# A fourth buffer for gathered rows during the gate-table stage, in the place of two extra raw buffers of U

## The chip, the cores and the metric

The kernel runs on one core of a Trainium2 chip. The metric is device time in microseconds (us). TensorE multiplies matrices (it takes its work from one sequencer, weight loads and matmuls in a row), VectorE and ScalarE work element by element, GpSimd here starts gathers, and SyncE's queue (SP) starts plain loads. Each engine works off its instructions in order.

## The reference, cut to what matters

One decoder layer on 528 tokens: a mixer (attention and mLSTM) and then a PEER layer, in which each token picks 128 of 16384 experts and uses a row of U and a row of V (2048 numbers each) of each expert:

```python
    idx = jnp.take_along_axis(cand_i, best_pos, axis=-1).reshape(T, PEER_HEADS * PEER_TOPK)
    gate = jax.nn.softmax(best_s, axis=-1).reshape(T, PEER_HEADS * PEER_TOPK).astype(h.dtype)
    ...
        ub = jnp.take(u, ib, axis=0)
        act = jax.nn.gelu(jnp.einsum('td,tkd->tk', hb, ub), approximate=False)
        return jnp.einsum('tk,tkd->td', gb * act, jnp.take(v, ib, axis=0))
```

## The kernel before

The PEER layer is done in two ways at once. For 352 tokens (ND) all 16384 experts are computed densely on TensorE: U is read in 128 chunks of 1 MB and multiplied, and a table of gates (zero but for the 128 picked experts) then weighs the result before it is multiplied with V. For the last 160 tokens the picked rows are gathered instead: GpSimd starts an indirect DMA that fetches one row per partition (128 rows of 8 KB, 1 MB), and VectorE multiplies it with the token's vector (rows of U) or adds it to a sum (rows of V). These are the 320 jobs of the list `jobs`, in the order d (128), D (32), A (32), a (128).

A chunk of U comes in two halves of 512 KB. `split_half` (L76 to L82) takes each apart for exact products: the load `raw` on SP's queue (L73), a cast `hi` on ScalarE (L80), and the subtraction `lo = raw - hi` on VectorE (L81), which is the last reader of `raw`. A chunk has 16 k-steps of three matmuls (L90 to L92: hi, lo, hi); the first half serves steps 0 to 7, the second 8 to 15. `step` (L888) first calls `uload` for the chunk after, then puts down its own matmuls; `u_chunk` (L899) adds a GELU on ScalarE (L902), which frees the PSUM bank, and a store.

`raw` tiles have 3 buffers in the pool `wp`. `hi` and `lo` have 5 each. Gathered rows (`ug`) have 3 buffers in the pool `gr`: `gather(j)` (L834) can start when the work on row j - 3 is done. `run(n)` (L861) puts down gathers up to three jobs ahead and the work until n jobs are done.

The gate-table stage (L1078 to L1144) is the part around the change. Its loop goes over chunks of U; after each chunk come up to two builds of gates for 4 tokens: `ebuild` (VectorE L1096 to L1099, ScalarE `ea` L1101), `gbuild` (12 small matmuls into `pg`, L1110), `gcopy` (ScalarE copies `pg` into `stg`, L1118; after 32 tokens the 2 MB of `stg`, which has one buffer, are stored to Gd in DRAM, L1120; there are 11 such stores). Then `pace(c)` runs as many jobs as bring their number to JU = 174 by the end of the loop. VectorE's, TensorE's and GpSimd's order is that of the program text here: the subtractions of the chunk after, then gates, then jobs. ScalarE's order is set by a planner when the kernel is built. Only in this stage is there a pool `ru` with two further `raw` buffers, which `uload` uses for two of five halves in turn, so that five raw buffers are in turn.

After the stage the last six chunks of U run beside the preparation of V; then V follows in 256 half tiles of the same kind, with the other jobs.

Of the kernel before, what the change touches and what calls it, by code (L numbers as in the profile page):

```python
# [8 lines left out]
F = mybir.dt.float32  # L9
# [10 lines left out]
D = 2048  # L20
# [40 lines left out]
def body(tc, I, out):  # L61
    nc = tc.nc
    top = ExitStack()
    with top:
# [206 lines left out]
        sP.close()  # L271
        L["sM"], L["sB"], L["big"] = sM, sB, big
        rest(tc, I, out, L)


# [391 lines left out]
def rest(tc, I, out, L):  # L667
    nc = tc.nc
    wp, dp, mixT, ident, nfw = L["wp"], L["dp"], L["mixT"], L["ident"], L["nfw"]
    split_half, load_half, split_tile, mm3, rsqrt_small, big = (  # L670
        L[n] for n in ("split_half", "load_half", "split_tile", "mm3", "rsqrt_small", "big"))
# [10 lines left out]
    w = {}  # L682
# [4 lines left out]
    with tc.tile_pool(name="op", bufs=1) as op_, tc.tile_pool(name="pso", bufs=6, space=PSUM) as pso:  # L687
# [34 lines left out]
        for i, (p, pr) in enumerate(seq):  # L722
            dc, tbs = passes[p]
            if pr == 0:
# [3 lines left out]
                ps = {tb: pso.tile([128, 512], F, name="po", tag="po") for tb in tbs}  # L728
# [7 lines left out]
            for j in range(2):  # L736
                n = 2 * pr + j
# [6 lines left out]
            if p == 4 and pr in (2, 5):  # L744
                b = stores.pop(0)
# [44 lines left out]
    for b in range(2):  # L790
        cs = slice(1024 * b, 1024 * b + 1024)
        t = wp.tile([128, 8, 128], F, name="nfr", tag="raw", bufs=3).rearrange("p a b -> p (a b)")
# [10 lines left out]
    gr = sG.enter_context(tc.tile_pool(name="gr", bufs=1, side="right"))  # L803
# [28 lines left out]
    rows, nj, acc, own = {}, [0, 0], {"d": h2n}, {"d": act, "D": actB, "a": act, "A": wB}  # L832

    def gather(j):  # L834
        kind, k = jobs[j]
        t = rows[j] = gr.tile([128, D], F, name="ug", tag="ug", bufs=3)
        ix = idx if kind in "da" else idxB
        nc.gpsimd.indirect_dma_start(out=t, out_offset=None, in_=I["un" if kind in "dD" else "vn"],  # L838
                                     in_offset=bass.IndirectOffsetOnAxis(ap=ix[:, k:k + 1], axis=0))

    def work(j):
        kind, k = jobs[j]
        t = rows.pop(j)
        o = own[kind][:, k:k + 1]
        if kind in "dD":
            nc.vector.scalar_tensor_tensor(t, t, 1.0, acc[kind], op0=OP.mult, op1=OP.mult, accum_out=o)  # L846
            if j in (127, 127 + SB):
                nc.scalar.activation(own[kind], own[kind], AF.Gelu)
            return
        if k == 0:  # L850
            if kind == "A":
                acc["A"] = gr2[0].tile([128, D], F, name="yB", tag="h2nB")
                nc.vector.tensor_tensor(wB, wB, actB, op=OP.mult)
                nc.vector.tensor_tensor(act, act, gsel, op=OP.mult)
            else:
                acc["a"] = gr.tile([128, D], F, name="y3", tag="h2n")
            nc.vector.tensor_scalar(acc[kind], t, o, None, op0=OP.mult)
        else:
            nc.vector.scalar_tensor_tensor(acc[kind], t, o, acc[kind], op0=OP.mult, op1=OP.add)  # L859

    def run(n, ready=NJ):  # L861
        while nj[1] < min(n, ready):
            while nj[0] < min(ready, nj[1] + 3):
                gather(nj[0])
                nj[0] += 1
            work(nj[1])
            nj[1] += 1
        while nj[0] < min(ready, nj[1] + 3):
            gather(nj[0])
            nj[0] += 1  # L870

    gr2 = []
    sp = [I["wq"][i] for i in range(16)] + [I["u"][c] for c in range(NK)]
    w[2] = split_tile(sp[2], "d2")

    ru = []

    def uload(n):
        if n < len(sp) and n not in w:
            ps = [None, None]  # L880
            if ru:
                for b in range(2):
                    if ru[1] % 5 in (1, 3):
                        ps[b] = (ru[0], 2)
                    ru[1] += 1
            w[n] = split_tile(sp[n], f"d{n}", ps)

    def step(n, mid=None):  # L888
        uload(n + 1)
        ps = pmu.tile([128, 512], F, name="pu", tag="pu")  # L890
        nn = S if n < 16 else ND
        for k in range(KD):
            mm3(ps[:, :nn], w[n], k, h2h, h2l, slice(0, nn))
            if k == 7 and mid:
                mid()
        w.pop(n)
        return ps

    def u_chunk(c, mid=None):  # L899
        ps = step(16 + c, mid)  # L900
        at = h2p.tile([128, ND], F, name="at", tag="at", bufs=3)
        nc.scalar.activation(at, ps[:, :ND], AF.Gelu)  # L902
        nc.scalar.dma_start(Ad[c // 4, :, c % 4, :], at)

    with tc.tile_pool(name="tk", bufs=1) as tk, \
# [116 lines left out]
        for n in range(2, 16):  # L1022
            ps = step(n, mid)
# [5 lines left out]
        while bg or pend or any(pipe):  # L1029
            u_chunk(ci, mid)  # L1030
            if ci % 2 and len(routed) > 1:
                run(nj[1] + 1, 16 * len(routed) - 16 if len(routed) < PH else 128)
            else:
                bgstep()
            ci += 1
# [24 lines left out]
        for src, dst in ((n1s, n1T), (n2s, n2T), (gs, None)):  # L1060
            pt = ptr.tile([128, ND], F, name="ptt", tag="ptt")
            for b in range(3):
                n = min(128, ND - 128 * b)
# [14 lines left out]
    with tc.tile_pool(name="gk", bufs=1, reuse_waits="tile") as gk, \  # L1078
            tc.tile_pool(name="psg", bufs=2, space=PSUM) as psg, \
            tc.manual_schedule(engines={mybir.EngineType.Pool}), \  # L1080
            tc.tile_pool(name="ru", bufs=1, reuse_waits="tile") as rup:
        stg, gd = {}, {}
        ru += [rup, 0]

        ge = {}

        def pairs(t):
            a = [list(p) for p in t.ap]
            return bass.AP(tensor=t.tensor, offset=t.offset, ap=[a[0], [2 * a[1][0], 2], [0, 128], [a[1][0], 2]])

        def ebuild(q):
            t0 = 4 * q
            e = gk.tile([128, 2, 2, 128, 2], BF, name="e", tag="e", bufs=2)
            eg = gk.tile([128, 2, 2, 128, 2], BF, name="eg", tag="eg", bufs=2)
            ea = gk.tile([128, 2, 2, 128], BF, name="ea", tag="ea", bufs=2)
            nc.vector.tensor_tensor(e[:, 0], iota2, pairs(n1T[:, t0:t0 + 4]), op=OP.is_equal)  # L1096
            nc.vector.tensor_tensor(e[:, 1], iota2, pairs(n2T[:, t0:t0 + 4]), op=OP.is_equal)
            for i in range(2):
                nc.vector.tensor_tensor(eg[:, i], e[:, 1], pairs(gp[:, 1 + i, t0:t0 + 4]), op=OP.mult)  # L1099
            for j in range(4):  # L1100
                nc.scalar.activation(ea[:, j // 2, j % 2, :], e[:, 1, j // 2, :, j % 2], AF.Copy,  # L1101
                                     scale=g0[:, t0 + j:t0 + j + 1])
            ge[q] = e[:, 0], [ea.rearrange("p a b n -> p a n b"), eg[:, 0], eg[:, 1]]

        def gbuild(q):
            e1, eg = ge.pop(q)
            pg = psg.tile([128, 4, 128], F, name="pg", tag="pg")
            for j in range(4):
                for i in range(3):
                    nc.tensor.matmul(pg[:, j, :], e1[:, j // 2, :, j % 2], eg[i][:, j // 2, :, j % 2],  # L1110
                                     start=(i == 0), stop=(i == 2))
            gd[q] = pg

        def gcopy(q):
            tg, r = divmod(4 * q, TG)
            if r == 0:
                stg[tg] = gk.tile([128, NK, TG], F, name="stg", tag="stg")
            nc.scalar.copy(stg[tg][:, :, r:r + 4], gd.pop(q).rearrange("p j n -> p n j"))  # L1118
            if r + 4 == TG:
                nc.scalar.dma_start(Gd[tg, :, 0:NK, :], stg[tg])  # L1120

        gr2.append(sG.enter_context(tc.tile_pool(name="gr2", bufs=1, side="right")))
        acc["D"] = gr2[0].tile([128, D], F, name="h2nB", tag="h2nB")
        for q in range(NQ):
            nc.scalar.dma_start(acc["D"][NB * q:NB * q + NB], hB)
        ng, n0, c0 = 0, nj[1], ci
        ebuild(0)

        def pace(c):
            run(n0 + int((c + 1 - c0) * (JU - n0) / (NK - UTAIL - c0)))  # L1130

        for c in range(ci, NK - UTAIL):
            u_chunk(c)
            while ng < min(ND // 4, (c + 1 - ci) * (ND // 4) / (NK - 17 - ci)):
                if ng - 1 in gd:
                    gcopy(ng - 1)
                gbuild(ng)
                ng += 1
                if ng < ND // 4:
                    ebuild(ng)  # L1140
            if ng == ND // 4 and gd:
                gcopy(ng - 1)
            pace(c)
        ru.clear()  # L1144
    sU.close()

    with ExitStack() as sV:
# [56 lines left out]
        for g in range(NG - 1):  # L1204
            n = GROUPS[g]
            free += [t0 + n + 2 * (j // 2) + 2 for j in range(n)]
            t0 += 2 * n
        for q in range(GROUPS[0], NK):
            g = max(x for x in range(NG) if g0s[x] <= q)
            m, n = q - g0s[g], GROUPS[g - 1]  # L1210
            base = 2 * g0s[g - 1]
            t = base + (2 * n * m) // GROUPS[g]
            t = max(t, free[q - AR] if q >= AR else 0, base - 4)
# [9 lines left out]
        for c in range(NK - UTAIL, NK):  # L1223
# [5 lines left out]
            for _ in range(-(-len(pro) // (NK - c))):  # L1229
                f, q = pro.pop(0)  # L1230
# [115 lines left out]
        for i, (g, hf, pr, c) in enumerate(vord[:last]):  # L1346
# [9 lines left out]
            if i == nlast - 8:  # L1356
                for b in range(2):
                    t = wp.tile([128, 8, 128], F, name="nlw", tag="raw", bufs=3)
# [22 lines left out]
            else:  # L1381
                dc = hf
                if pr == 0:
                    ps = []
# [10 lines left out]
                if tail:  # L1395
                    f, tb = tail.pop(0)
# [96 lines left out]
```

## Time and profile before

| | us |
|---|---|
| median of 3 runs | 3291.85 (3288.75 to 3292.93) |
| the profiled execution | 3289.89 |
| its span, first to last instruction | 3288.1 |
| TensorE busy in the span | 3222.9 (98%) |
| VectorE busy | 2323.8 (71%) |

The profile is one execution; 1.8 us of its time lie outside the span. Busy times of an engine are summed over its instructions; matmuls overlap, so a busy TensorE is not one at its peak. The granted clock is the share of TensorE's full 2.4 GHz that it was given.

### The profile page before, as it was taken

The numbers are of one execution on the slowest core, as the hardware profiler recorded it, in microseconds if no ns is written. First come the engines' busy times: TensorE is split into PE (matmuls) and PEld (weight loads), VectorE is DVE, ScalarE is ACT, GpSimd is POOL, SyncE is SP. The second block draws the span as 40 slices with busy tenths as digits, with TensorE's granted clock in tenths as the row PEclk, the third lists the DMA queues.
The fourth block names the chain that finished last, engine by engine and source line by source line (L and its number), as shares of the span: only waits on it lengthen the run. The fifth ranks groups of instructions, "written<-read, shape, count | busy, mean of one in ns | idle before, by whom it ended". The sixth has DMA issues, their size and how long they took to land.

```text
span 3288.1 us, 51152 instructions
## 1 busy us (share of the span) xinstructions
PE 3222.9 (98%) x20174; PEld 3038.4 (92%) x20174; DVE 2323.8 (71%) x3521; ACT 1315.1 (40%) x2219; POOL 932.0 (28%) x974
## 2 busy tenths in 40 slices
PE   8999999999999999999999999999999999999998
PEld 7889898888887899999999999999999999999997
DVE  7444444444266688888988889876787888887875
ACT  5444544444252233354544444434333333333323
POOL 2011111110007666523333344331222222222212
PEclk9999999999999999999999999999999999999999
DMA  4222122223363256679999999998998988988973
GB/s 156 71 71 78 65 72 71 65 71 109 109 211 126 90 194 220 239 285 374 388 364 389 374 367 391 388 413 292 374 336 334 373 324 332 375 320 330 362 277 139
DMA packets 230161, 815.47 MB, mean 248 GB/s; under 512 B 21696, under 2 KB 85696, under 8 KB 186528
## 3 DMA queue, kind: packets, MB, share of 16 engines
q1 hardware_dynamic: 103904, 377.65, 31.9%
q0 software_dynamic: 46080, 335.56, 26.0%
q10 hardware_dynamic: 79936, 98.98, 8.6%
q8 instruction: 158, 2.59, 0.3%
q14 instruction: 83, 0.68, 0.1%
HBM read 757.33 MB, written 54.79 MB: 247 GB/s over the span
## 4 chain that ended last, share of the span: by engine, by line
PE 64%; issue 18%; POOL 10%; DVE 4%; DMA 3%; ACT 1%; ACTq 0%; POOLq 0%; SPq 0%; DVEq 0%
PE py L1304 9%; PE py L1306 9%; PE py L1305 9%; POOL ug L838 8%; PE ps L90 6%; PE ps L92 5%; PE ps L91 5%; PE pu L90 3%; PE pu L91 3%; PE pu L92 3%; PE po L743 2%; PE po L741 2%; PE po L742 2%; DMA ug<-in_vn_dram,idxB 1%; PE pn L534 1%
## 5 line engine op out<-in xcount | busy, mean ns | idle before, releaser
L91 PE MATMUL pu<-hh,lod 128*128 128x352 f32 (+1 forms) x2272 | 756.2, 333 | 16.7 <-DVE lod L81 16.6
L90 PE MATMUL pu<-hh,hid 128*128 128x352 f32 (+1 forms) x2272 | 763.8, 336 | 2.7 <-ACT at L902 2.7
L92 PE MATMUL pu<-hl,hid 128*128 128x352 f32 (+1 forms) x2272 | 754.0, 332 | 0.0
L1305 PE MATMUL py<-ah,lov 128*128 128x352 f32 x1984 | 641.4, 323 | 5.8 <-DVE lov L81 5.8
L1304 PE MATMUL py<-ah,hiv 128*128 128x352 f32 x1984 | 644.4, 325 | 0.6 <-ACT at L902 0.6
L1306 PE MATMUL py<-al,hiv 128*128 128x352 f32 x1984 | 643.8, 325 | 0.0
L80 ACT CAST hiv<-rawv 128x1024 fp32r<-128x1024 f32 x256 | 269.0, 1051 | 549.6 <-PE py L1306 482.6
L91 PEld LDWEIGHTS pu<-hh,lod 128*128 128x128 f32 x2272 | 431.1, 190 | 27.9 <-DVE lod L81 18.5
L90 PEld LDWEIGHTS pu<-hh,hid 128*128 128x128 f32 x2272 | 431.8, 190 | 12.6 <-ACT at L902 3.0
L92 PEld LDWEIGHTS pu<-hl,hid 128*128 128x128 f32 x2272 | 431.0, 190 | 9.8
L81 DVE TENSOR_TENSOR lod<-rawd,hid 128x1024 fp32r<-128x1024 f32 x284 | 363.0, 1307 | 70.6 <-ACT hid L80 70.4
L90 PE MATMUL ps<-xh,hiz 128*128 128x256 f32 (+2 forms) x1280 | 410.3, 321 | 0.6 <-DVE qT L370 0.5
L92 PE MATMUL ps<-xl,hiz 128*128 128x256 f32 (+2 forms) x1280 | 392.5, 307 | 0.0
L91 PE MATMUL ps<-xh,loz 128*128 128x256 f32 (+2 forms) x1280 | 392.0, 306 | 0.0
L838 POOL DMA_INDIRECT ug<-in_vn_dram,idx x128 | 208.3, 1627 | 618.6 <-DVE y L859 598.2
L80 ACT CAST hid<-rawd 128x1024 fp32r<-128x1024 f32 x284 | 295.7, 1046 | 211.5 <-PE pu L92 109.2
L1305 PEld LDWEIGHTS py<-ah,lov 128*128 128x128 f32 x1984 | 372.7, 188 | 7.9 <-DVE lov L81 7.9
L1304 PEld LDWEIGHTS py<-ah,hiv 128*128 128x128 f32 x1984 | 372.8, 188 | 0.8 <-ACT at L902 0.8
L1306 PEld LDWEIGHTS py<-al,hiv 128*128 128x128 f32 x1984 | 372.0, 187 | 0.0
L838 POOL DMA_INDIRECT ug<-in_un_dram,idx x128 | 249.7, 1951 | 404.4 <-DVE ug L846 386.1
L81 DVE TENSOR_TENSOR lov<-rawv,hiv 128x1024 fp32r<-128x1024 f32 x256 | 311.8, 1229 | 64.3 <-ACT hiv L80 64.3
L846 DVE SCALAR_TENSOR_TENSOR ug<-ug,h2n 128x2048 f32<-128x2048 f32 x128 | 304.2, 2396 | 39.3 <-DMA ug<-in_un_dram,idx 39.0
(343 smaller groups left out, 4845.8 us busy)
## 6 DMA issues: line engine op xcount, KB each, us to landing
rawd<-in_u_dram SPq DMA_DIRECT2D x256, 512.0 KB, 7.5
rawv<-in_v_dram SPq DMA_DIRECT2D x256, 512.0 KB, 6.6
rawz<-in_wz_dram SPq DMA_DIRECT2D x98, 512.0 KB, 3.6
Ad<-at ACTq DMA_DIRECT2D x128, 176.0 KB, 6.2
Gd<-stg ACTq DMA_DIRECT2D x11, 2048.0 KB, 15.9
gt<-Gd ACTq DMA_DIRECT2D x32, 704.0 KB, 12.2
av<-Ad ACTq DMA_DIRECT2D x64, 352.0 KB, 6.7
rawwo<-in_wo_dram SPq DMA_DIRECT2D x40, 512.0 KB, 3.8
```

The lines of the kernel that those rows point to most:

```text
L80: nc.scalar.copy(hi, raw)
L81: eng.tensor_tensor(lo, raw, hi.bitcast(F), op=OP.subtract)
L90: nc.tensor.matmul(ps, a, xh[k][:, cs], start=(k == 0), stop=False)
L91: nc.tensor.matmul(ps, b, xh[k][:, cs], start=False, stop=False)
L92: nc.tensor.matmul(ps, a, xl[k][:, cs], start=False, stop=(k == KD - 1))
L741: nc.tensor.matmul(ps[tb], mh[n][:, sl], h, start=(n == 0), stop=False)
L742: nc.tensor.matmul(ps[tb], mh[n][:, sl], l, start=False, stop=False)
L838: nc.gpsimd.indirect_dma_start(out=t, out_offset=None, in_=I["un" if kind in "dD" else "vn"], in_offset=bass.IndirectOffsetOnAxis(ap=ix[:, ...
L846: nc.vector.scalar_tensor_tensor(t, t, 1.0, acc[kind], op0=OP.mult, op1=OP.mult, accum_out=o)
L1304: nc.tensor.matmul(po, h, ah, start=(pr + j == 0), stop=False)
L1305: nc.tensor.matmul(po, l, ah, start=False, stop=False)
L1306: nc.tensor.matmul(po, h, al, start=False, stop=(2 * pr + j == n - 1))
```

## The change

In the gate-table stage the pool `ru` no longer holds two raw buffers but one `ug` buffer. Every fourth gathered row (j % 4 == 3) goes there, the others to the three buffers of `gr`, so gathers go up to four jobs ahead; `room()` says whether the next row's pool has a free buffer, and `home[j]` whether row j is in `gr`. `uload` uses the three raw buffers of `wp` throughout. When the loop ends, jobs go on until no row that is still to be worked on lies in `ru`.

```diff
 def gather(j):
         kind, k = jobs[j]
-        t = rows[j] = gr.tile([128, D], F, name="ug", tag="ug", bufs=3)
+        pool, n = (ru[0], 1) if ru and j % 4 == 3 else (gr, 3)
+        home[j] = pool is gr
+        t = rows[j] = pool.tile([128, D], F, name="ug", tag="ug", bufs=n)
...
     def run(n, ready=NJ):
         while nj[1] < min(n, ready):
-            while nj[0] < min(ready, nj[1] + 3):
+            while nj[0] < ready and room():
                 gather(nj[0])
                 nj[0] += 1
             work(nj[1])
             nj[1] += 1
-        while nj[0] < min(ready, nj[1] + 3):
+        while nj[0] < ready and room():
             gather(nj[0])
             nj[0] += 1
 
-    gr2 = []
+    gr2, ru, home = [], [], {}
+
+    def room():
+        in_gr = not (ru and nj[0] % 4 == 3)
+        return sum(home[j] == in_gr for j in range(nj[1], nj[0])) < (3 if in_gr else 1)
...
-    ru = []
-
     def uload(n):
         if n < len(sp) and n not in w:
-            ps = [None, None]
-            if ru:
-                for b in range(2):
-                    if ru[1] % 5 in (1, 3):
-                        ps[b] = (ru[0], 2)
-                    ru[1] += 1
-            w[n] = split_tile(sp[n], f"d{n}", ps)
+            w[n] = split_tile(sp[n], f"d{n}")
...
-        ru += [rup, 0]
+        ru.append(rup)
...
         ru.clear()
+        while not all(home[j] for j in range(nj[1], nj[0])):
+            run(nj[1] + 1)
     sU.close()
```

## Rows read from the trace of the kernel before

**Rows 1.** Windows: length, busy us (PE PEld DVE ACT POOL), clock, DMA share, GB/s

```profile
1660.00:1720.00 60.00, 54.48 (x373) 53.33 (x372) 51.43 (x66) 26.46 (x53) 22.58 (x13) 0.94 0.98 383
1420.00:2210.00 790.00, 768.15 (x5364) 755.46 (x5364) 686.81 (x836) 367.76 (x708) 302.73 (x159) 0.98 0.97 379
2120.00:2210.00 90.00, 87.99 (x544) 87.69 (x543) 71.30 (x52) 26.68 (x33) 29.63 (x21) 1.00 1.02 413
2360.00:3200.00 840.00, 840.00 (x5185) 840.00 (x5184) 684.22 (x650) 271.28 (x313) 208.90 (x129) 1.00 0.91 340
1170.00:1420.00 250.00, 250.00 (x1547) 249.85 (x1546) 209.62 (x497) 91.81 (x138) 130.93 (x226) 1.00 0.64 223
```

**Rows 2.** Waits of TensorE, 1420 to 2210: us, times, longest

```profile
PE pu L91 <- DVE lod L81: 16.6, 6, 5.5
```

**Rows 3.** Timelines of ScalarE, VectorE and TensorE around one store

```profile
1660.94 1.04 ACT L80 CAST hid<-rawd 128x1024 fp32r<-128x1024 f32 x1
1663.66 0.33 ACTq L1120 DMA_DIRECT2D Gd<-stg  x1
1670.78 1.04 ACT L80 CAST hid<-rawd 128x1024 fp32r<-128x1024 f32 x1
...
1680.35 2.29 DVE L846 SCALAR_TENSOR_TENSOR ug<-ug,h2n 128x2048 f32<-128x2048 f32 x1 [6.26 <-DMA ug<-in_un_dram,idx]
1682.57 2.36 DVE L81 TENSOR_TENSOR lod<-rawd,hid 128x1024 fp32r<-128x1024 f32 x2
...
1683.84 0.66 PE L91 MATMUL pu<-hh,lod 128*128 128x352 f32 x1 [5.52 <-DVE lod L81]
```

**Rows 4.** Groups by line, 1420 to 2210: busy us, mean ns, idle before and what ended it

```profile
L846 DVE SCALAR_TENSOR_TENSOR ug<-ug,h2n 128x2048 f32<-128x2048 f32 x113 | 255.9, 2287 | 39.3 <-DMA ug<-in_un_dram,idx 39.0
L81 DVE TENSOR_TENSOR lod<-rawd,hid 128x1024 fp32r<-128x1024 f32 x181 | 213.6, 1220 | 8.7 <-ACT hid L80 8.7
L80 ACT CAST hid<-rawd 128x1024 fp32r<-128x1024 f32 x180 | 187.4, 1046 | 121.4 <-DMA rawd<-in_u_dram 72.9 <-PE pu L92 47.6 <-ACT hid L80 0.6
L846 DVE SCALAR_TENSOR_TENSOR ug<-ug,h2nB 128x2048 f32<-128x2048 f32 x32 | 72.8, 2288 | 20.0 <-DMA ug<-in_un_dram,idxB 20.0
L902 ACT ACTIVATE at<-pu 128x352 f32<-128x352 f32 x90 | 41.1, 457 | 113.5 <-PE pu L92 113.3
L859 DVE SCALAR_TENSOR_TENSOR yB<-ug,wB,yB 128x2048 f32<-128x2048 f32 x13 | 30.6, 2350 | 8.0 <-DMA ug<-in_vn_dram,idxB 7.9
```

**Rows 5.** DMA issues, 1420 to 2210: count, KB each, median us to landing

```profile
DMA packets 64493, 299.44 MB, mean 379 GB/s; under 512 B 7009, under 2 KB 19910, under 8 KB 42911
...
rawd<-in_u_dram SPq DMA_DIRECT2D x179, 512.0 KB, 8.5
Gd<-stg ACTq DMA_DIRECT2D x11, 2048.0 KB, 15.9
```

**Rows 6.** DMA issues in three store windows: 1480 to 1496, 1664 to 1680, 2118 to 2134

```profile
rawd<-in_u_dram SPq DMA_DIRECT2D x2, 512.0 KB, 13.2
...
rawd<-in_u_dram SPq DMA_DIRECT2D x2, 512.0 KB, 16.8
...
rawd<-in_u_dram SPq DMA_DIRECT2D x4, 512.0 KB, 13.9
```

**Rows 7.** Line 838 (the gathers), 1420 to 2210: its landings

```profile
DMA to landing us min/median/max: 7.0/9.9/17.0
```

**Rows 8.** DMA issues before the stage, 1170 to 1420

```profile
rawd<-in_u_dram SPq DMA_DIRECT2D x64, 512.0 KB, 4.0
```

**Rows 9.** DMA issues behind the last store, 2135 to 2206

```profile
rawd<-in_u_dram SPq DMA_DIRECT2D x16, 512.0 KB, 9.4
```

**Rows 10.** Waits of all engines behind the stage, 2210 to 2240

```profile
DVE lod L81 <- ACT hid L80: 12.3, 7, 6.0
PE pu L90 <- ACT at L902: 2.7, 1, 2.7
```

## The prediction

> **What bounds the kernel now.** I read the windows by stage first. Before the gate-table stage TensorE is busy 250 of 250 us, in the V stage 840 of 840, but from 1420 to 2210 us, where the changed lines act, 768.15 of 790 [rows 1]. A change there can pay only where TensorE waits, 21.85 us, or runs at its lower clock. The waits of TensorE name most of it: 16.6 us in six waits for `lod`, VectorE's subtraction in `split_half` [rows 2]. Two stretches of 60 us, 1660 to 1720 and one like it from 1840, show a granted clock of 0.94 [rows 1]. TensorE's longest wait for `lod`, 5.52 us, lies in the first [rows 3], so the lower level (1.2 instead of 2.4 GHz) goes with a long wait here.
>
> Why is `lod` late? The timeline shows the worst place: VectorE, whose order is written by hand, stands 6.26 us for a gathered row, then does the two subtractions that stood behind it, and TensorE starts 5.52 us late; counted from the stage's start, the casts of this pair are those at 1660.94 and 1670.78, long done [rows 3]. In sum VectorE stands 39.0 + 20.0 + 7.9 = 66.9 us for gathered rows in the stage, and only 8.7 us for casts [rows 4]. Just before, at 1663.66 us, ScalarE had issued a Gd store of 2 MB [rows 3]; such a store takes 15.9 us to land, against 8.5 for a raw half of U and 9.9 for a gather (medians) [rows 5, 7]. So eleven times in the stage a store makes everything land late, and what has the least lead stops VectorE. The DMA engines are near full: 0.97 of them busy, and 1.02 behind the last gates [rows 1].
>
> **The change, part by part.** Instructions, bytes and SBUF stay as they are: one tile of 8 KB per partition replaces two of 4 KB. Only leads move.
>
> Gathers. A gather starts when VectorE has worked off the row three jobs back. The stage does 113 + 32 + 13 jobs and one first row of V, 159 in 790 us [rows 4], one per 5.0 us, and a job takes 2.3 us. The lead is 3 x 5.0 - 2.3 = 12.7 us now, 17.7 with four buffers; the longest landing of the stage is 17.0 [rows 7]. I take the 66.9 us of waiting to vanish; bounds: all of it, or none where a deeper queue lands later by as much as it starts earlier. With it the six waits for `lod` go: 16.6 us. The two stretches at 0.94 give back 0.06 x 60 = 3.6 us each, if no other long wait takes their place: 7.2 us. Together 23.8 us at most.
>
> Raw halves. Their buffers go in turn, two per chunk of U, and each is freed by its own subtraction; five are in turn now, three after. A chunk lasts 790 / 90 = 8.8 us (90 GELUs [rows 4]). Say that the first subtraction of chunk n starts at T; it ends at T + 1.2. With three buffers that frees the tile for the second half of chunk n + 1, whose subtraction is due at T + 8.8 + 1.2 and whose cast takes 1.05 us before it: the load may take 8.8 + 1.2 - 1.2 - 1.05 = 7.7 us. The first half of chunk n + 1 waits for the second subtraction of chunk n - 1 and may take 17.6 - 2.4 - 1.05 = 14.1. With five buffers both have 8.8 us more, 16.5 and 22.9. So second halves become what has the least lead. Before the stage three raw buffers were enough, because loads landed in 4.0 us [rows 8].
>
> What that costs. The stage's median landing, 8.5 us, is over both halves; of each two loads that are freed 1.2 us apart the later stands behind the earlier in the queue, and the earlier is the one with 7.7 us. Outside the stores I take no wait. Of the eleven store windows nine tell a median: seven of them 12.5 to 16.8 (mean 14.1; three of them stand in the rows), two about 7 [rows 6]. Late by 14.1 - 7.7 = 6.4 us in 7/9 of eleven stores: 8.6 x 6.4 = 55 us. Behind the last store the chunks have no gate work and raws land in 9.4 us with the DMA engines full [rows 9]; nine chunks, late by half of 9.4 - 7.7 = 1.7 us to all of it: 8 to 15 us. VectorE's new waiting is 63 to 70 us, say 68, against 66.9 removed. Bounds: 0, if loads speed up where no gather hurries; and 11 x (16.8 - 7.7) + 15 = 115.
>
> What stands behind the new wait: ScalarE waits at its cast, and behind it on ScalarE stand `ea` (TensorE's gate matmuls wait for it), the GELU that frees a PSUM bank, and the issue of stores; VectorE stands behind the cast with gates and jobs. SP's queue holds nothing but raw loads in this stage. TensorE has some more cover than today: it needs a second half only after eight of sixteen k-steps. I take today's conversion: 66.9 us of VectorE's waiting cost 16.6 + 7.2 = 23.8 us, 0.36 each. So 68 cost 24.5, net +0.7. The bounds cost 0 and 41: net -23.8 and +17.
>
> End of the stage. `run` goes on until no row sits in the extra buffer: jobs 174 and 175, 2 x 2.35 us of VectorE [rows 4], come before the next chunk's subtractions instead of in V. VectorE has no gates to build there; cost 0, or 4.7 if its lead is gone. V loses two jobs where TensorE is never idle [rows 1]: 0. I add 2.5 us for this and for casts that block ScalarE.
>
> Sum: 3289.9 - 23.8 + 24.5 + 2.5 = 3293.1, against the profiled execution of 3289.89, which lies 2 us under the median of the runs, 3291.85. **I forecast 3293 us.** A difference of 0.2%, 6.6 us, is about what can be told from none: the limits are 3285.3 and 3298.4.
>
> The Trainium skill bears on the step that keeps today's landing times for raws. In the store windows three queues have work at once, and a raw takes 12.5 to 16.8 us [rows 6] instead of 4.0 [rows 8]. "DMA: Bandwidth & Descriptors", section "Queues, rings and completion order", says that a DMA engine takes one packet from a ring and goes on to the next ring that has work. By that rule one more gather in the gathers' own ring takes no turn from the raws, and the sum stays as above; were it one line for all, 1 MB more ahead, at 379 GB/s, would make each raw land 2.8 us later, and late casts (below) would be the likely case. No row here tells the two apart.
>
> **Rivals.**
> *The raw slack holds* (faster). Loads speed up where gathers need not hurry, and second halves are late by less than the half-chunk that TensorE covers. For it: that cover, and that with three raw buffers and landings of 4.0 us TensorE was busy throughout [rows 1, 8]. Against: seven stores with 12.5 to 16.8 us [rows 6]. Gain 9 to 23.8 us: 3266 to 3281, middle 3274.
> *Late casts block ScalarE* (slower). One place has three raw buffers and busy DMA engines: behind the stage VectorE waited 12.3 us for casts, and TensorE 2.7 us for a GELU that stood behind a cast in ScalarE's order [rows 10]. If the stores do the same on top of the forecast, 1 to 11 times 2.7 us: 3296 to 3323, middle 3308. It decides where second halves land later than 7.7 + 4.4 us (half a chunk is TensorE's cover) after their issue.
> *The DMA engines are the bound, and moving buffers does nothing*: 3290. For it: the share of 0.97. Against: 299 MB [rows 5] at the 413 GB/s of the last stretch [rows 1] is 725 us, 65 below the stage's 790. The Trainium skill, "Trainium Kernel Development and Optimization", section "Key Constraints", states that DMAs from all issuing engines interleave on the same 16 DMA engines; taken alone, that would give this case.
>
> **Chances.** Forecast (the waits change place, 3281 to 3305): 0.36, of it 0.06 faster, 0.20 same, 0.10 slower. Raw slack holds: 0.28, all faster. Late casts: 0.30, of it 0.01 same, 0.29 slower. DMA bound: 0.06, same. So faster 0.34, same 0.27, slower 0.39. The range, 3266 to 3320, holds the first rival but for its low end and the second but for its top; some 2 in 10 stay out.
>
> **What the profile after would show.** Right: VectorE's waits for gathered rows from 66.9 us to under 10; ScalarE's wait for raws well over its 72.9 [rows 4]; VectorE's wait for casts from 8.7 to between 50 and 90; TensorE's idle time in the stage within 8 us of 21.85. The raw slack holding would show under 30 us of VectorE's waits for casts and a clock of 1.00 throughout; late casts would show TensorE waiting over 30 us for `ea`, the GELU and `lod` together. I am wrong if gathers land later by the 5 us that they gain, or if ScalarE's new order puts work that TensorE needs in every chunk behind the casts.

## The result and the profile after

The changed kernel takes 3329.28 us (median of 4 runs, 3326.90 to 3334.56), the kernel before 3290.30 us beside it (3283.13 to 3292.93). The ratio is 1.0123, with a 95% interval of 1.0110 to 1.0136: slower by 1.2%, about 40 us. 3293 was forecast, with a range up to 3320.

Where the 39.3 us between the two profiled spans (3327.4 and 3288.1 us) lie can be read from the eleven gate stores. One line of each trace gives the count of the stores and the start of the first and the last, before and then after:

```profile
L1120 ACTq DMA_DIRECT2D Gd<-stg x11: 326/327/327, 1479.8 to 2118.4; - x11
```

```profile
L1119 ACTq DMA_DIRECT2D Gd<-stg x11: 326/326/327, 1484.2 to 2154.7; - x11
```

Up to the first store after is 4.4 us later. From first to last it takes 670.5 instead of 638.6 us, 31.9 more (a mean of 3.2 for each of ten intervals). Behind the last store 1172.7 us are left instead of 1169.7, 3.0 more. 4.4 + 31.9 + 3.0 = 39.3: the loss lies in the gate-table stage, spread over the stretches between its stores (all but one of the ten are longer, by 0.4 to 6.9 us), and hardly any at its end. The stage now ends near 2250 us, so the views of after are taken up to there.

The windows say the same (columns as in [rows 1]), after and then before:

```profile
1420.00:2210.00 790.00, 742.23 (x5163) 726.66 (x5162) 659.80 (x818) 359.20 (x696) 304.92 (x152) 0.97 0.94 363
1420.00:2250.00 830.00, 778.47 (x5385) 762.60 (x5383) 691.95 (x836) 370.35 (x710) 322.48 (x161) 0.97 0.94 364
```

```profile
1420.00:2250.00 830.00, 805.46 (x5585) 792.47 (x5585) 707.45 (x862) 384.23 (x732) 302.73 (x159) 0.98 0.96 376
```

TensorE stands for 51.5 of 830 us instead of 24.5, and its granted clock falls from 0.98 to 0.97. The DMA engines moved less per us than before (364 instead of 376 GB/s): they are not what got full.

The waits of after in 1420 to 2250 us (us, times, longest):

```profile
ACT hid L80 <- DMA rawd<-in_u_dram: 302.7, 135, 7.3
DVE lod L81 <- ACT hid L80: 122.8, 55, 7.9
ACT stg L1117 <- DMA Gd<-stg: 72.9, 9, 11.2
...
PE pg L1109 <- DVE lod L81: 18.2, 2, 11.7
PE pg L1109 <- ACT ea L1100: 18.1, 11, 6.1
...
PE pu L90 <- ACT at L901: 7.2, 5, 4.4
...
PE pg L1109 <- DVE eg L1098: 3.7, 3, 2.6
...
DVE yB L861 <- DMA ug<-in_vn_dram,idxB: 2.1, 1, 2.1
```

What the change was to remove is removed: VectorE's waits for gathered rows fall from 66.9 us [rows 4] to 2.1. But its waits for casts rise from 8.7 + 12.3 = 21.0 us [rows 4, 10] to 122.8, and ScalarE's for raws from 82.1 us in the same stretch (72.9 up to 2210 us [rows 4]) to 302.7. TensorE's waits, 16.6 us for `lod` at L91 before [rows 2], are now at the gate matmuls (`pg`) and at the GELU.

DMA issues of the stage after, for [rows 5]; in the median raws land about as fast after their issue as before (8.6 us for 8.5):

```profile
DMA packets 63994, 302.29 MB, mean 364 GB/s; under 512 B 7080, under 2 KB 19020, under 8 KB 42060
...
rawd<-in_u_dram SPq DMA_DIRECT2D x180, 512.0 KB, 8.6
Gd<-stg ACTq DMA_DIRECT2D x11, 2048.0 KB, 16.8
```

The dearest place, behind the first store, in the timelines of ScalarE, VectorE and TensorE:

```profile
1484.16 0.33 ACTq L1119 DMA_DIRECT2D Gd<-stg  x1
...
1487.68 1.05 ACT L80 CAST hid<-rawd 128x1024 fp32r<-128x1024 f32 x1 [1.59 <-DMA rawd<-in_u_dram]
1499.81 0.59 ACT L1117 COPY stg<-pg 128x512 f32<-128x512 f32 x1 [11.07 <-DMA Gd<-stg]
1500.29 1.99 ACT L80 CAST hid<-rawd 128x1024 fp32r<-128x1024 f32 x2
1502.18 1.28 ACT L1100 ACTIVATE ea<-e,g 128x128 bf16<-128x128 bf16 x4
...
1501.37 2.36 DVE L81 TENSOR_TENSOR lod<-rawd,hid 128x1024 fp32r<-128x1024 f32 x2 [6.24 <-ACT hid L80]
...
1502.64 0.26 PE L1109 MATMUL pg<-ea,e 128*128 128x128 bf16 x1 [11.75 <-DVE lod L81]
```

The copy into `stg` waits 11.07 us for the store, behind it stand two casts and `ea`; VectorE waits 6.24 us for those casts, TensorE 11.75 us for both. Its granted clock around the end of this wait is 0.50, the lower level of 1.2 GHz:

```profile
1495.50:1505.80 10.30, 3.16 (x19) 3.16 (x19) 3.95 (x7) 4.78 (x9) 0.84 (x1) 0.50 1.00 418
```

So a first reading is that the copy's wait for the store is the cause. The experiments show that the loss stays when this wait is taken away.

### The profile page after: what moved, and what is told of

It reads as the page before. It is cut to its first block, busy times and chain, and to the rows that moved or that the text cites. A ratio compares the mean times of both kernels' runs of the same rounds, so it can differ in the third digit from the quotient of the medians.

```text
span 3327.4 us, 51115 instructions
## 1 busy us (share of the span) xinstructions
PE 3231.1 (97%) x20170; PEld 3044.0 (91%) x20174; DVE 2326.3 (70%) x3521; ACT 1317.5 (40%) x2219; POOL 948.9 (29%) x974
## 3 DMA queue, kind: packets, MB, share of 16 engines
q1 hardware_dynamic: 103904, 377.65, 31.7%
## 4 chain that ended last, share of the span: by engine, by line
PE 64%; DMA 14%; DVE 11%; issue 5%; ACT 3%; POOL 2%; ACTq 0%; SPq 0%; POOLq 0%; DVEq 0%
DMA rawd<-in_u_dram 9%; PE py L1307 9%; PE py L1305 9%; PE py L1306 9%; PE ps L90 5%; PE ps L92 5%; PE ps L91 5%; PE pu L90 4%; PE pu L91 4%; PE pu L92 4%; DVE ug L848 3%; DMA Gd<-stg 3%; DVE lod L81 3%; PE po L743 2%; PE po L741 2%
## 5 line engine op out<-in xcount | busy, mean ns | idle before, releaser
L91 PE MATMUL pu<-hh,lod 128*128 128x352 f32 (+1 forms) x2272 | 756.3, 333 | 4.5 <-DVE lod L81 4.5
L91 PEld LDWEIGHTS pu<-hh,lod 128*128 128x128 f32 x2272 | 431.8, 190 | 14.6 <-DVE lod L81 5.1
L91 PE MATMUL ps<-xh,loz 128*128 128x256 f32 (+2 forms) x1280 | 391.8, 306 | 0.0
L840 POOL DMA_INDIRECT ug<-in_vn_dram,idx x128 | 208.7, 1631 | 627.0 <-DVE y L861 608.0
## 6 DMA issues: line engine op xcount, KB each, us to landing
Gd<-stg ACTq DMA_DIRECT2D x11, 2048.0 KB, 16.8
```

What stands on the lines that cost most here:

```text
L91: nc.tensor.matmul(ps, b, xh[k][:, cs], start=False, stop=False)
```

## The experiments

Each kernel was timed in 5 rounds beside the kernel before, whose median was 3285.4 to 3290.1 us there; ratios are taken against those runs of before. "Tight" kernels have one `lo` and one `at` buffer less. The last three columns are read from each run's windows and waits, 1420 to 2250 us: time in which TensorE is not busy, VectorE's waits for casts (us, longest), ScalarE's waits for raws. This window is the same for all, so in a faster kernel it holds more of what follows the stage; and they come from one execution each, which can lie some us off the median (e6 3281.9, e11 3310.5, e17 3334.9 us).

| kernel | median us | ratio [95%] | TensorE stands | casts | raws |
|---|---|---|---|---|---|
| before | 3290.3 | 1 | 24.5 | 21.0, 6.0 | 82.1 |
| after | 3329.3 | 1.0123 [1.0110, 1.0136] | 51.5 | 122.8, 7.9 | 302.7 |
| e1 raws 3, gathers 3 | 3331.1 | 1.0133 [1.0116, 1.0150] | 54.5 | 99.3, 6.7 | 299.7 |
| e2 raws 4, gathers 3 | 3294.8 | 1.0023 [1.0012, 1.0033] | 28.4 | 31.7, 6.9 | 234.5 |
| e3 raws 5, gathers 4, tight | 3263.4 | 0.9925 [0.9912, 0.9938] | 7.3 | 23.1, 3.3 | 121.0 |
| e4 before, tight | 3274.3 | 0.9962 [0.9948, 0.9976] | 15.6 | 15.4, 3.8 | 86.9 |
| e5 after, stores gone | 3278.2 | 0.9965 [0.9953, 0.9978] | 14.0 | 72.0, 4.8 | 361.9 |
| e6 after, small stores | 3274.4 | 0.9950 [0.9937, 0.9964] | 18.1 | 77.2, 4.2 | 337.0 |
| e16 before, small stores | 3252.0 | 0.9901 [0.9886, 0.9916] | 2.0 | 8.5, 4.0 | 64.1 |
| e9 after, stores from DRAM | 3338.6 | 1.0155 [1.0137, 1.0174] | 49.2 | 140.6, 14.7 | 291.9 |
| e10 before, stores from DRAM | 3276.8 | 0.9966 [0.9951, 0.9980] | 21.7 | 38.6, 7.9 | 68.7 |
| e11 raws 3, gathers 3, tight | 3321.2 | 1.0098 [1.0080, 1.0116] | 44.4 | 90.8, 6.5 | 307.6 |
| e12 e11 with two `stg` | 3317.2 | 1.0086 [1.0067, 1.0105] | 50.3 | 96.4, 6.0 | 365.5 |
| e15 after, stores halved | 3308.7 | 1.0074 [1.0060, 1.0087] | 40.3 | 113.6, 5.9 | 391.3 |
| e7 after, second half later | 3330.7 | 1.0127 [1.0112, 1.0143] | 46.9 | 108.9, 12.0 | 287.1 |
| e8 after, ScalarE in text order | 3339.5 | 1.0154 [1.0140, 1.0168] | 45.1 | 142.4, 9.1 | 132.8 |
| e13 after, `ea` on VectorE | 3328.4 | 1.0132 [1.0116, 1.0147] | 45.9 | 108.8, 7.0 | 406.7 |
| e14 before, `ea` on VectorE | 3292.9 | 1.0021 [1.0012, 1.0030] | 29.7 | 12.4, 7.3 | 153.3 |
| e17 after, end not flushed | 3323.2 | 1.0097 [1.0080, 1.0114] | 51.1 | 134.8, 7.4 | 308.5 |
| e18 e3 with stores halved | 3260.5 | 0.9906 [0.9890, 0.9923] | 4.2 | 4.3, 1.6 | 160.3 |

### Which half of the change costs (e1 to e4)

e1 takes the raw buffers away and leaves the gathers at three:

```diff
-            ps = [None, None]
-            if ru:
...
-            w[n] = split_tile(sp[n], f"d{n}", ps)
+            w[n] = split_tile(sp[n], f"d{n}")
```

> One half of the change alone: the two extra raw buffers are gone (three raw buffers), the gathered rows keep their three. Theory A (the lost lead of the raw halves is the cost: late casts in ScalarE's order stop VectorE and TensorE): slower than before by at least the 39 us of the changed kernel, 3325 to 3350, with ScalarE's wait for raws near 300 us and VectorE's waits for casts over 100 us in the stage. Rival B (the fourth gather in flight costs, by filling the DMA engines' queues): within 10 us of before, 3283 to 3300. Rival C (the end of the stage, where jobs are worked off early, costs): as B.

Slower by 1.33%, 43.7 us (38 to 49): the raw buffers alone cost all of the loss, and the fourth gather buffer gives back 0.10%, 3 us, with intervals that overlap. Rivals B and C fall.

e2 leaves one extra raw buffer (`if ru[1] % 4 == 1: ps[b] = (ru[0], 1)`):

> One extra raw buffer instead of two, three gather buffers. Theory A: a load of a half then may take about 12 us instead of 7.7 (three buffers) or 16.5 (five), so part of the loss: 3298 to 3320, between before and the kernel with three raws, and ScalarE's wait for raws between 73 and 303 us. Rivals B and C: as before, 3283 to 3298.

0.23%, 8 us, under the expected range: one buffer takes away some 36 of 44 us. The "about 12 us" of the expectation was reckoned wrongly. By the prediction's own way a half's buffer is freed, with four in turn, by the same half two chunks before: 17.6 - 1.2 - 1.05 = 15.3 us for both halves. Three buffers give 7.7 and 14.1; so the fourth doubles the shorter lead, to above most of the store windows (mean 14.1, [rows 6]), and the fifth adds little to it (16.5).

e3 has all five raws and four gather buffers; the room comes from one `lo` and one `at` buffer less. e4 is the control:

```diff
-            lo = wp.tile([128, 8, 128], R, name="lo" + name, tag="wlo")
+            lo = wp.tile([128, 8, 128], R, name="lo" + name, tag="wlo", bufs=4)
...
-        at = h2p.tile([128, ND], F, name="at", tag="at", bufs=3)
+        at = h2p.tile([128, ND], F, name="at", tag="at", bufs=2)
```

> The other half alone: the fourth gather buffer beside both extra raw buffers; the room is found by taking one of five lo buffers and one of three at buffers away in the whole kernel. Theory A: the gather waits (66.9 us) go and nothing takes their place, so the 16.6 us of TensorE's waits for lod and some of the clock come back: 3266 to 3282, faster than the kernel with the same room taken away. Rival B: slower than that kernel by 20 us or more. Rival D (the gather waits were free, what is removed there is worth nothing): within 5 us of it.

> The kernel before with one of five lo buffers and one of three at buffers taken away, and nothing else: the control for the kernel with five raws and four gathers. All theories: 3285 to 3300; above that, the buffers taken away cost by themselves, and the comparison goes against this time.

The control missed its range: it is 0.38% faster than before. Most of that lies ahead of the stage; from 600 to 1170 us TensorE is busy 567.06 instead of 558.41 us. Why was not tried. Against the control the fourth gather buffer gives 0.37%, 12 us, half of the 23.8 predicted. VectorE's waits for rows fall from 67.7 (37.4 + 21.4 + 8.9) to 13.8 us, and its waits for casts rise by 7.7. The waits of VectorE and TensorE that matter, e4 and then e3:

```profile
DVE ug L846 <- DMA ug<-in_un_dram,idx: 37.4, 17, 7.3
...
PE pu L91 <- DVE lod L81: 12.4, 6, 4.4
```

```profile
DVE ug L848 <- DMA ug<-in_un_dram,idx: 9.0, 7, 1.8
...
PE pu L91 <- DVE lod L81: 3.2, 2, 3.1
```

TensorE's waits for `lod` fall by 9.2 us; the mean clock of the profiled execution is 0.993 in both, so the clock gave nothing that shows. With the fourth gather buffer raws land later, 10.8 us for 8.7; the rows are those of the DMA issues, 1420 to 2250 us, e4 and then e3:

```profile
rawd<-in_u_dram SPq DMA_DIRECT2D x181, 512.0 KB, 8.7
```

```profile
rawd<-in_u_dram SPq DMA_DIRECT2D x181, 512.0 KB, 10.8
```

### What the stores have to do with it (e5, e6, e16, e9 to e12, e15)

e5 lets the store take its bytes from U in DRAM, e6 stores 4 of 128 columns:

```diff
-                nc.scalar.dma_start(Gd[tg, :, 0:NK, :], stg[tg])
+                for i in range(4):
+                    nc.scalar.dma_start(Gd[tg, :, 32 * i:32 * i + 32, :],
+                                        I["u"][2 * tg + i // 2][i % 2].rearrange("p (k t) -> p k t", t=TG))
```

> The changed kernel, but each 2 MB store of gates takes its bytes from U in DRAM instead of from stg (as four DMAs of 512 KB): the gate table in DRAM is not the computed one, the bytes moved stay, and ScalarE's copy into stg no longer waits for the store. Theory A1 (part of the loss is the copy that stands 8 to 11 us behind each store, with casts, ea and GELU behind it in ScalarE's order, and no cast done ahead): ScalarE's 72.9 us for the store go, 3300 to 3318. Theory A2 (the loss is raws that land later than the 7.7 us lead, store or not): 3322 to 3332.

> The changed kernel with stores of 4 of 128 gate columns (64 KB instead of 2 MB), and V reading these four alone: most gates are left out, and 22 of 302 MB in the stage. Takes away the copy's wait and the store's load on the DMA engines together. A1: as the run with the bytes kept, 3300 to 3318. A2 with the stores as what makes raws late, as the prediction had it (loss only in store windows): 3275 to 3295. A2 with raws late in every chunk: 3305 to 3325, and ScalarE still waits over 200 us for raws.

e5 did not do what its expectation says. Nothing ties these DMAs to the stage, and the planner issued all of them in the first 300 us; that stretch's DMA issues have the row

```profile
Gd<-in_u_dram ACTq DMA_DIRECT2D x44, 512.0 KB
```

So in both runs the stores' bytes and the copy's wait are gone together, and both come out below before, 3278 and 3274. ScalarE still waits over 330 us for raws and VectorE 72 to 77 us for casts there, at little cost to TensorE (14 and 18 us). A long sum of waits for raws is not the loss by itself.

e16 is the same edit as e6 on the kernel before:

> The kernel before with stores of 4 of 128 gate columns (64 KB instead of 2 MB), and V reading these four alone: most gates are left out. It prices the stores for five raws as the run of the changed kernel with small stores (3274, 55 us under its own) does for three. Theory L: five raws take up most of the stores, so the gain here is 15 to 25 us, to 3264 to 3275, and without stores both kernels are within 10 us of each other. Rival (three raws are short with or without stores): 3240 to 3262.

It gains 0.99%, 33 us, more than Theory L had: the time lies in the rival's range. After gains 1.23 + 0.50 = 1.73%, 57 us. So of the 40 us between the two kernels 57 - 33 = 24 come with the stores, and 0.9950 - 0.9901 = 0.49%, 16 us, stay without them: L and its rival each have a part. The first to last store times (line as above; e6, e16) put the parts at about half each: 627.0 and 611.6 us, 15.4 apart, for 31.9 with stores.

```profile
L1119 ACTq DMA_DIRECT2D Gd<-stg x11: 326/327/348, 1482.7 to 2109.7; - x11
```

```profile
L1120 ACTq DMA_DIRECT2D Gd<-stg x11: 326/326/327, 1474.5 to 2086.1; - x11
```

Is it the copy that waits, or the bytes? e9 and e10 put DRAM-to-DRAM copies of about the same bytes at the store's place, from a block of Ad just written:

```diff
-                nc.scalar.dma_start(Gd[tg, :, 0:NK, :], stg[tg])
+                for i in (0, 44, 84):
+                    nc.scalar.dma_start(Gd[tg, :, i:i + 44, :],
+                                        Ad[c // 4 - 1].rearrange("p a n -> p (a n)").rearrange("p (k t) -> p k t", t=TG))
```

> The changed kernel, with each store of gates replaced at its place by three copies of 0.72 MB inside DRAM, out of the block of Ad that was just finished (the gate table in DRAM is not the computed one). So the store's bytes and their time in the stage stay, and stg's copy waits for no store. Theory W (the copy that waits for the store holds up ScalarE, and all that stands behind it): 3272 to 3292, about as with the stores gone from the stage (3278 and 3274). Theory L (the store's bytes make raws land late for three buffers): 3310 to 3330.

> The same edit on the kernel before: five raws, three gather buffers, bytes of the stores kept, no wait of the copy. Theory W: ScalarE's 47.8 us of waiting there did little harm, since two chunks were cast ahead: 3275 to 3292, a gain of 0 to 15 us, far from the 40 us of the changed kernel. Theory L: no change, 3284 to 3294.

After does not recover at all, which speaks for L; before gains 0.34%, inside W's range and under L's. The pair is not clean: ScalarE now stood for the copies themselves (e9):

```profile
ACT ea L1100 <- DMA Gd<-Ad: 50.9, 6, 12.7
```

e12 is cleaner. `stg` gets a second buffer (`bufs=2`) in the room of the `ru` pool and the tight buffers; in the stage ScalarE's order is that of its control e11 but for one `ea` and the copy beside it.

> Control for the next: three raws, three gather buffers, four lo buffers and two at buffers in the whole kernel. All theories: 14 us under the 3331 of three raws and three gathers, if the gain of the tight control (3274 against 3288) is outside the gate-table stage: 3310 to 3325.

> As the control, and stg with two buffers of 16 KB per partition in the room of both extra tiles, so that the copy after a store need not wait for it; nothing else changes, ScalarE's order included, and every value is computed. Theory W: 3265 to 3285, about 40 us under the control, though raws keep three buffers and ScalarE's wait for them stays near 300 us. Theory L: within 10 us of the control.

ScalarE's 70.5 us of waiting for the store in e11 are gone, and the time is the same (intervals overlap; 4 us between the medians). Theory W falls: without the copy's wait the loss is still there. What took the copy's place stands in e12's timelines of ScalarE, VectorE and TensorE behind the same first store:

```profile
1470.46 0.33 ACTq L1114 DMA_DIRECT2D Gd<-stg  x1
...
1475.62 0.58 ACT L1112 COPY stg<-pg 128x512 f32<-128x512 f32 x1
1481.49 1.04 ACT L80 CAST hid<-rawd 128x1024 fp32r<-128x1024 f32 x1 [5.30 <-DMA rawd<-in_u_dram]
1488.46 1.04 ACT L80 CAST hid<-rawd 128x1024 fp32r<-128x1024 f32 x1 [5.92 <-DMA rawd<-in_u_dram]
...
1489.54 1.23 DVE L81 TENSOR_TENSOR lod<-rawd,hid 128x1024 fp32r<-128x1024 f32 x1 [5.74 <-ACT hid L80]
...
1489.86 0.27 PE L1104 MATMUL pg<-ea,e 128*128 128x128 bf16 x1 [11.76 <-ACT ea L1095]
```

The copy runs at once, at 1475.62, and TensorE still waits 11.76 us, for 11.75 in after: two casts, 5.30 and 5.92 us late with their raws, do what the copy did. Both waits end about when the store's bytes are through (an estimate for e12: 1470.46 + 16.8, the store's median landing in after, is 1487.3); to take one away leaves the other.

That the stores make raws late is seen in their windows. In the first window of after, 1484 to 1500 us, raws take 15.0 us; in e16, 1480 to 1496, 5.1:

```profile
rawd<-in_u_dram SPq DMA_DIRECT2D x2, 512.0 KB, 15.0
```

```profile
rawd<-in_u_dram SPq DMA_DIRECT2D x4, 512.0 KB, 5.1
```

Nine windows of after have a median, 6.4 to 16.1, mean 12.8 us; the nine of before, three of them in [rows 6], have a mean of 12.5. Of e16 the windows were taken where before's stores lie, not at its own small ones; ten have a median, 5.1 to 11.0, mean 8.4.

e15 gathers 16 tokens per store and has two `stg` buffers of half the size (`TG = 16`):

> The changed kernel with gates gathered for 16 tokens instead of 32 per store: 22 stores of 1 MB in the place of 11 of 2 MB, from two stg buffers of half the size in the same room. Every value is computed; V reads the table in pieces of half the length. Theory L (a store's bytes make raws land later than three buffers allow): 1 MB delays a raw by half as much, so most store windows fall under the lead: 3290 to 3312. Rival (the bytes count, not their size at once, or three raws are short anyway): 3322 to 3340.

0.49% better than after, 16 us of the 57 that the stores cost there. The bytes are the same, so their number alone is not what counts. But the copy's wait for the store is gone here too. e12 prices that at nothing beside stores of 2 MB, where the late raws land about when the copy's wait would have ended; beside stores of 1 MB it was not tried alone. How the 16 us are shared between the smaller store and the second `stg` buffer is open.

### Does the order of the engines matter (e7, e8, e13, e14)

e7 puts the second half's cast and subtraction behind the gate work:

```diff
+            raws = [load_half(sp[n][b], f"d{n}_{b}") for b in range(2)]
+            w[n] = [split_half(None, f"d{n}_0", raws[0])]
+            late.append((n, raws[1]))
...
+            second()
             pace(c)
```

> The changed kernel with the cast and subtraction of the second half of a chunk put down after the gate work of the chunk before, ahead of the jobs, instead of straight behind the first half's; loads stay in their order. The second half's subtraction moves back by about x = 3 us of VectorE's gate work, so its load may take 7.7 + x and the first half's 14.1 - x. Theory A2 (the lead of second halves is what is short): ScalarE's wait for raws falls well under 303 us, 3295 to 3315. Rival (three buffers are too few however they are spaced, or the later subtraction is itself late for TensorE): 3325 to 3340.

e8 adds ScalarE to the engines whose order is the program text's:

> The changed kernel with ScalarE's instructions of the stage in the order of the program text instead of the planner's: both casts of a chunk, then GELU, copy into stg, ea. The leads of the raws stay at 7.7 and 14.1 us. If what hurts TensorE is the first-half cast that the planner puts ahead of stg and ea, TensorE's waits for ea and GELU (25 us) shrink to under 10 and the time falls to 3300 to 3318. If it is VectorE's wait for casts in its own order, nothing changes: 3322 to 3340.

e13, and e14 on before, make `ea` a third product on VectorE:

```diff
-            for i in range(2):
-                nc.vector.tensor_tensor(eg[:, i], e[:, 1], pairs(gp[:, 1 + i, t0:t0 + 4]), op=OP.mult)
-            for j in range(4):
-                nc.scalar.activation(ea[:, j // 2, j % 2, :], e[:, 1, j // 2, :, j % 2], AF.Copy,
...
+            for i in range(3):
+                nc.vector.tensor_tensor(eg[:, i], e[:, 1], pairs(gp[:, i, t0:t0 + 4]), op=OP.mult)
```

> The changed kernel with ea made by VectorE as a third product beside eg (87 instructions of about 0.42 us, 37 us more for VectorE) instead of by ScalarE (351 instructions, 115.6 us less). Every value is computed. Theory S (late casts reach TensorE through ScalarE's order: ea stands behind a cast that waits for a late raw): the waits of TensorE for ea are gone and what is left is its wait for VectorE: 3295 to 3318. Theory V (they reach it through VectorE's order: gates and subtractions behind a subtraction that waits for its cast, and 37 us more work there): 3325 to 3350.

> The same edit on the kernel before, as a control: casts are two chunks ahead there, so ScalarE's order does little harm, and VectorE has 37 us more work. Theory S: 3282 to 3300. Theory V: 3290 to 3310.

None helps: 1.27, 1.54 and 1.32% for 1.23%. In e7 ScalarE's wait for raws hardly falls (287.1 us) and TensorE's moves from the gates to the chunks, so it is not shown that the second halves' lead alone is what is short; in e8 TensorE still waits 21.9 us for `ea`. With `ea` off ScalarE the waits of TensorE took other names (e13):

```profile
PE pg L1105 <- DVE eg L1097: 15.1, 7, 3.6
PE pu L90 <- ACT at L901: 12.1, 9, 5.2
...
PE pu L91 <- DVE lod L81: 6.7, 9, 1.1
```

Theory S falls as the one route; the edit costs 0.21% on before, so moving `ea` was worth about 0.1%, no more than the intervals tell apart.

### The end of the stage, and a better version (e17, e18)

e17 stops using the extra buffer two jobs before the end (`j < JU - 2`), so nothing is worked off early:

> The changed kernel, but the extra buffer takes no row after job 171, so nothing has to be worked off early when the stage ends. Prediction's step for the end of the stage: jobs 174 and 175 cost 0, or 4.7 us if VectorE's lead is gone: 3324 to 3332. Rival C (the end of the stage is a good part of the loss): 3300 to 3322.

0.26% under after, 9 us, with intervals that just overlap: not settled by the times. In its trace, that of its longest execution, 1170.2 us are left behind the last store (2162.9 of 3333.1), for 1172.7 in after, 1169.7 in before and 1175.2 in e1, which has no such end (2153.6 of 3328.8). So the traces show no cost of this end that stands out from such differences of a few us.

e18 is e3 with `TG = 16` and two `stg` buffers:

> Five raws and four gather buffers in the room of one lo and one at buffer (3263), with the stores halved and stg in two buffers of half the size. What the runs point to: five raws take up a store of 1 MB fully and the copy waits for none, so part of the 33 us that stores cost the kernel before comes back: 3245 to 3260. If V pays for the shorter pieces in which it reads the table: 3260 to 3275, with the gain in the stage and the loss in V.

3260.5 us, 0.94% faster than before (0.77 to 1.10%), the fastest that computes everything; against e3 the intervals overlap. The second of the two expectations is the nearer: up to the last store e18 is 8.0 us ahead of e3 (2085.9 for 2093.9 us), and behind it takes 6.8 longer (1174.3 for 1167.5). TensorE is busy 825.76 of 830 us with the DMA engines at 0.97.

## Why the prediction was wrong

**Gathers, the gain of 23.8 us: the waits vanished as said, the price was too high.** 66.9 us of waits went to 2.1. Where raws have their five buffers that is worth 12 us (e3 against e4), the step "With it the six waits for `lod` go" nearly right (9.2 us of 12.4) and the 7.2 us from the clock not seen. With three raws it is worth about 3 us (after against e1), which the intervals do not tell from nothing: VectorE's waits for rows fall from 39.9 us to 2.1, but its waits for casts rise from 99.3 to 122.8. The prediction added the two terms as if each acted alone.

**Raws, the loss of 24.5 us: 43.7 was measured (e1).** The landing times taken over from before hold over both halves: a median of 8.6 us for 8.5, and store windows with a mean of 12.8 for 12.5. The Trainium skill, "DMA: Bandwidth & Descriptors", section "Queues, rings and completion order", was cited for this step: a DMA engine takes a packet from one ring and goes on to the next that has work. The runs do not settle what that makes of a fourth gather: with three raw buffers raws land in 8.6 us with it and 8.2 without (after, e1), with five in 10.8 and 8.7 (e3, e4), for the 2.8 us that the prediction worked out for one line. Two steps behind it failed:

- "Outside the stores I take no wait" is refuted by e6: with small stores VectorE waits 77.2 us for casts, for 8.5 in e16, and the two kernels are 16 us apart. The reason given, that the loads with 7.7 us land earlier than the median says, held for before and not for after. Followed load by load, as far as the traces allow (about half of them), second halves land in a median of 7.1 us in before and 8.1 in after, outside the store windows 7.1 and 7.9: over their lead of 7.7.
- "I take today's conversion", 0.36 us for each us that VectorE waits, is not one number. In e1 VectorE waits 78.3 us more for casts, near the 68 taken, and the kernel takes 43.7 us longer: 0.56 each. The gather waits cost 12 / 53.9 = 0.2 (e3, e4). Without large stores the casts' 68.7 us more cost 16, 0.2 each, though 34.9 us of waits for rows go at the same time (e16, e6). With them after waits 45.6 us more for casts than e6 (122.8 - 77.2) and takes 57 us longer, more than one for one. So 41 us for the bound of 115 was too low.

**The end of the stage, 2.5 us:** 3.0 more than before lie behind the last store, but 5.5 more in e1, which has no such end, and 0.5 in e17. No run shows this term by itself.

**The rivals.** The DMA engines as the bound is refuted by e16 and e18. The raw slack holding is refuted by the casts' waits. Late casts had the sign, its condition (landing above 12.1 us: seven of nine store windows) and its mark: TensorE waits 18.2 + 18.1 + 7.2 us for `lod`, `ea` and the GELU, over 30. Its price, 2.7 us a store taken from [rows 10], was too small: the 36 us over the forecast are 3.3 for each of eleven stores, and the dearest single wait took 11.75 us. That is why the range ended at 3320. It was also not the stores alone: 16 of the 40 us stay without them. Its route through ScalarE alone is not borne out (e13): the late raw holds ScalarE and VectorE, and whatever is freed of one waits on the other. How the price is shared between the two is open.

## What to carry to other kernels

Work out for each buffer how long its transfer may take, and compare that with the landing times in the worst windows and with the median: a reckoned 7.7 us beside medians of 8.6 (after) and 8.8 (e16) cost 16 us even without large stores, 15.3 us cost 8 in all. Do not carry one price for a us of waiting over from one kernel to the next: here it went from 0.2 to over 1. And where two waits end with the same event, a profile names the one that ended last; only taking it away (a second `stg` buffer) tells whether the loss needs it.

## What was not expected

The kernel before with two kinds of buffer cut (e4) is 0.38% faster, with TensorE 8.65 us busier from 600 to 1170 us; it was not followed up. The stores, 23 of 302 MB in the stage of after, cost the kernel before 33 us (the traces of before and e16 have 27.0 of it between the first and the last store) though its engines move 376 GB/s with them and 361 without. That speaks for late landings, not the throughput, as what TensorE pays for.
